# Bias sums dealt to a later stretch of each token group, and the first key weights split after the first group's input, in a two-layer GLA and stick-breaking kernel

## The chip, the core and the metric

The kernel runs on one NeuronCore of one Trainium2 chip. The metric is the device time of one execution in microseconds (us); lower is better. Five engines work beside one another and each takes its own instructions in order: TensorE (PE, with PEld for its weight loads), VectorE (DVE), ScalarE (ACT), GpSimd (POOL), and SyncE (SP), which issues nearly all transfers.

## The reference

There are 2048 tokens of 1024 features, in float32. Layer 0 is gated linear attention with 4 heads, layer 1 is stick-breaking attention with 16 heads whose keys and values come from a second modulated norm of the same stream. Every norm is scaled and shifted by vectors computed from a condition `c`.

```python
def ada_modulate(c, w, b, n):
    cond = jax.nn.silu(c) @ w + b
    return jnp.split(cond[:, None, :], n, axis=-1)
...
    proj = h @ w_in
    q, k, v, g, gk_lr = jnp.split(proj, GLA_SPLITS, axis=-1)
    gk = jax.nn.log_sigmoid((gk_lr @ w_gk2 + b_gk).astype(f32)) / GLA_GATE_NORMALIZER
...
    o = rms_norm(o, o_gain).reshape(bsz, seq, GLA_VAL_DIM) * jax.nn.silu(g.astype(f32))
    return o.astype(h.dtype) @ w_out
...
    q, g = jnp.split(h @ w_in, 2, axis=-1)
```

## The kernel before, in words

**Precision.** A weight or an activation is kept as two pieces, a high one made by ACT (`AF.Copy` into the rounded type) and a low one made by DVE (value less high piece). A product is then three matmuls (`mm3`, lines 142 to 144). `load_split` (L116 on ACT, L117 on DVE) does this to a weight block of two halves, each of which is one transfer `wr_*` issued by SP and two tiles `wh_*` and `wl_*` from a pool of ten (`wsp`).

**Layer 0** goes through four token groups of 512 (`g` = 0 to 3). For each group and each of 4 heads, `qkv` makes value, key and query projections (`pv`, `pk`, `pq`), `gate` the decays, `gla` the attention, `out_gate` the gate projection (`pg`), and `out_proj` the output (`py`). Within `gla`, the squares of the head's output are summed on ACT and DVE (`ss_o`, L192 to L196), and `rstd` feeds the sum to one matmul on PE (`ms_o`, L211), which stands five steps after the squares whatever the engines do meanwhile. While a group's first heads are projected, `normed_out` finishes the group before (`x` L577, `x1n` L222 and L223, stored by SP as `xn`).

**Bias sums.** In groups 2 and 3 `bias_sums` computes what the norm's shift adds to layer 1's projections: for each of 8 head pairs it loads the pair's weights in two halves (`wb`, issued by SP at L672), sums them on DVE over 8 rows of weights (`bs`, L686 once and L688 seven times), and `total` adds up over the partitions: two PE transposes (`pb`, L665) and one DVE reduction into `biases` (L667). Group 2 does the key and value weights, group 3 the query and gate weights. The `wb` tiles come from the same pool `wsp` as the weight pieces, and `pb` takes a bank of the same pool of four (`pl`) as `pv`, `pk`, `pq`, `ms_o` and `py`.

**What sets the order.** PE's order is the order of the program text: `play` advances the main work one step at a time (a step is usually three or six matmuls) and after each step each side job that was given to `spawn(gen, delay, every)`: it starts `delay` steps later and moves once in `every` steps. The other engines' orders are made by a list scheduler with priorities, in which work under `urgent()` goes early and work under `relaxed(n)` goes late; the bias sums are under `relaxed(200)`. Only `start()` is written out for all of PE, ACT, DVE and SP: there the text's order holds. It computes the first group's condition and its normed input `h_0` to `h_7` (`scaled`, L330 and L331; low piece L339). Weights are fetched one block ahead: `next_weight` takes the one in the list `ahead` and appends the next.

Of the kernel before, what the change touches and what calls it, by code (L numbers as in the profile page):

```python
# [1 line left out]

# [32 lines left out]
def yoco_kernel(ctx: ExitStack, tc: tile.TileContext, I: dict, O: dict):  # L35
# [20 lines left out]
    def t2(name, dt=F32):  # L56
        return m2.tile([P, TG], dt, tag="m2", name=name)
# [147 lines left out]
    def rstd(name, sq, mean, n=TG):  # L205


        ms = bank(po, f"ms_{name}")[:, 0:n]
        sq = sq if isinstance(sq, list) else [sq]
        for i, x in enumerate(sq):  # L210
            nc.tensor.matmul(ms, mean, x, start=i == 0, stop=i == len(sq) - 1)  # L211
        r = t2(f"r_{name}")[:, 0:n]
        q = t2(f"rq_{name}")[:, 0:n]
        nc.scalar.activation(r, ms, AF.Ln, bias=epsc)
        nc.scalar.activation(r, r, AF.Exp, scale=-0.5)
        nc.scalar.activation(q, r, AF.Square)
        nc.vector.scalar_tensor_tensor(q, ms, epsc, q, op0=ALU.add, op1=ALU.mult)
        nc.vector.scalar_tensor_tensor(r, q, -3.0, r, op0=ALU.add, op1=ALU.mult)
        return r
# [6 lines left out]
    def ada_rows(name, w, j, pool):  # L226

        acc = t4(f"aa_{name}_{j}", [P, D])
        for kt in range(KT):
            raw = pool.tile([P, D], F32, tag=pool.name, name=f"wa_{name}_{j}_{kt}")  # L230
            nc.sync.dma_start(raw, w[kt * P:(kt + 1) * P, j * D:(j + 1) * D])
            s = s_col[:, kt:kt + 1]
            if kt == 0:
                nc.vector.tensor_scalar(acc, raw, s, None, op0=ALU.mult)
            else:
                nc.vector.scalar_tensor_tensor(acc, raw, s, acc, op0=ALU.mult, op1=ALU.add)
            yield
        return acc
# [33 lines left out]
    def load_x(g, i, name="x"):  # L272
        t = t4(f"{name}_{g}_{i}", [P, 2, TG])
        nc.sync.dma_start(t, I["x"][g][:, 2 * i:2 * i + 2, :])
        return [t[:, 0], t[:, 1]]
# [24 lines left out]
    def start():  # L300

        T = start_group(0)
        w = I["w_ada"][0]
        rows = [ada_rows("l0", w, j, act) for j in range(2)]
        xs, sq = [], []
        for i in range(4):
            xs += load_x(0, i)
            for kt in (2 * i, 2 * i + 1):
                sq.append(t2(f"sq_x0_{kt}"))
                nc.scalar.activation(sq[kt], xs[kt], AF.Square)  # L310
        for _ in range(6):
            next(rows[0])
        r = rstd("x0", sq, mean_d)
        cond, pcs = new_cond("l0", 2), []
        for j in range(2):
            acc = result(rows[j])
            if j:
                gate_weights()
                ahead.append(next(blocks))
            pcs.append(bank(po, f"pc_l0_{j}"))  # L320
            ada_sum(pcs[j], acc)
        for j in range(2):
            cols = slice(8 * j, 8 * j + 8)
            nc.vector.tensor_tensor(cond[:, cols], pcs[j][:, 0:8], b_ada[:, cols], op=ALU.add)
        a, b = mods["l0m"] = modulation("l0", norm_gain[:, 0:8], cond)

        def scaled(kt):
            h = new_h(0, kt)
            xn = t2(f"xn_0_{kt}")
            nc.vector.scalar_tensor_tensor(xn, xs[kt], a[:, kt:kt + 1], r, op0=ALU.mult, op1=ALU.mult)  # L330
            nc.scalar.activation(h[:, 0], xn, AF.Identity, bias=b[:, kt:kt + 1])  # L331
            return h, xn

        ready = [scaled(0)]
        for kt in range(KT):
            if kt + 1 < KT:
                ready.append(scaled(kt + 1))
            h, xn = ready[kt]
            nc.vector.scalar_tensor_tensor(h[:, 1], xn, b[:, kt:kt + 1], h[:, 0].bitcast(F32),  # L339
                                           op0=ALU.add, op1=ALU.subtract)  # L340
            T.hs.append((h[:, 0], h[:, 1]))
        return T


# [241 lines left out]
    def start_group(g):  # L586
        T = Piece()
        T.g, T.hs, T.G, T.on, T.sg, T.og = g, [], {}, {}, {}, []
        return T
# [16 lines left out]
    blocks = weight_blocks()  # L606
    ahead = []

    def next_weight():
        if not ahead:  # L610
            ahead.append(next(blocks))
        w = ahead.pop()
        n = next(blocks, None)
        if n is not None:
            ahead.append(n)
        return w

    sides = []
# [1 line left out]
    def spawn(gen, delay=0, every=1):  # L620

        sides.append([gen, delay, every])
        return gen
# [32 lines left out]
    def bias_sums(i):  # L656


        which, m = (("w_kv", "kvm"), ("w_qg", "l1m"))[i]
        b = mods[m][1]  # L660

        def total(p, acc):
            pb = bank(po, f"pb_{i}_{p}")[:, 0:2 * P]
            for j in range(2):
                nc.tensor.transpose(pb[:, j * P:(j + 1) * P], acc[:, j * P:(j + 1) * P], ident)  # L665
            at = 4 * p + 2 * i
            nc.vector.tensor_reduce(biases[:, at:at + 2], pb.rearrange("p (j t) -> p j t", j=2),  # L667
                                    axis=mybir.AxisListType.X, op=ALU.add)

        def load(p, hf):  # L670
            raw = wsp.tile([P, 4, 256], F32R, tag="wsp", name=f"wb_{i}_{p}_{hf}").bitcast(F32)
            nc.sync.dma_start(raw, I[which][p][:, 4 * hf:4 * hf + 4, :])  # L672
            return raw

        seq = [(p, hf) for p in range(SBP) for hf in range(2)]
        raw, before = load(*seq[0]), None
        for n, (p, hf) in enumerate(seq):
            yield
            if hf == 0:
                acc = t2(f"bs_{i}_{p}")[:, 0:2 * P]  # L680
            with relaxed(200):
                for j in range(4):
                    kt = 4 * hf + j
                    s = b[:, kt:kt + 1]
                    if kt == 0:
                        nc.vector.tensor_scalar(acc, raw[:, j], s, None, op0=ALU.mult)  # L686
                    else:
                        nc.vector.scalar_tensor_tensor(acc, raw[:, j], s, acc, op0=ALU.mult, op1=ALU.add)  # L688
            if hf == 0 and before:
                total(*before)  # L690
            before = p, acc
            if n + 1 < len(seq):
                raw = load(*seq[n + 1])
        yield
        total(*before)

    def layer0():
        with tc.manual_schedule(engines={PE, ACT, DVE, mybir.EngineType.SP}):
            T = start()
        after = iter(())  # L700
        slow = ada("g0", I["w_ada"][0], b_ada, 2, 1)
        for g in range(NG):
            T.ready = 0
            first = qkv(T, 0)
            for _ in gate_low_rank(T):
                if g == 0:
                    next(first)
            spawn(slow, 1, 9)
            spawn(call(gate, T, 0), 3)
            spawn(after, 10, 2)  # L710
            extra = spawn(bias_sums(g - 2), 10, 12) if g > 1 else iter(())
            mix, gat = spawn(heads(T)), spawn(gates(T))
            N = start_group(g + 1) if g + 1 < NG else None
            for h, g_h in ((0, ()), (1, ()), (2, (0,)), (3, (1, 2, 3))):
                if h + 1 < GH:
                    spawn(call(gate, T, h + 1), 14)
                yield from first if h == 0 else qkv(T, h)
                spawn(is_ready(T), 6)
                for i in g_h:
                    if i == 2 and N:  # L720
                        spawn(squares_in(N), 8, 1)
                    yield from out_gate(T, i)
            run(mix)
            run(gat)
            into = normed_in(N) if N else prepare_pair(0)
            spawn(into, 2, 4 if N else 3)
            yield from out_proj(T)
            run(into)
            run(slow)
            run(extra)  # L730
            after = normed_out(T)
            if g == 0:
                slow = ada("kv", I["kv_w_ada"], kv_b_ada, 0, 2)
            if g == 1:
                mods["kvm"] = modulation("kv", kv_gain, mods["kv"])
                slow = ada("l1", I["w_ada"][1], b_ada[:, 24:48], 0, 3)
            if g == 2:
                mods["l1m"] = modulation("l1", norm_gain[:, 8:16], mods["l1"])
                mods["g1"] = mods["l1"][:, 16:24]
            T = N  # L740
        last.append(after)
# [391 lines left out]
```

## Time and profile before

| | |
|---|---|
| median of 3 runs | 2678.39 us (2674.71 to 2679.36) |
| the profiled execution | 2672.68 us |
| its span in the trace | 2670.9 us |
| mean granted TensorE clock | 0.987 of full speed |
| PE, DVE, ACT busy | 97%, 80%, 57% of the span |

The span is what the trace shows; about 2 us lie around it. Layer 0 takes the first 970 us or so, group 2 starts near 500 us and group 3 near 745 us. Since PE is busy nearly all the time, its idle time, and the time after it in which its clock is low, are what a change of order can take away or add.

### The profile page before, as it was taken

The page shows a single profiled execution, that of the slowest core. Times are in us where ns is not written, and L with a number is a line of the kernel's source. Part 1 is how long each engine was busy: PE and PEld are TensorE (multiplying, and loading weights), DVE is VectorE, ACT ScalarE, POOL GpSimd, SP SyncE. Part 2 cuts the span into 40 slices and gives each one's busy share as a digit, 9 for nine tenths or more (in the row PEclk, how much of TensorE's full clock was granted, in tenths as well). Part 3 has the DMA queues.
Part 4 walks back from the last instruction along what each step waited for, and adds up shares of the span by engine and source line. Part 5 has one row for each costly group of instructions (what it writes and reads, how often), then busy time and mean ns, then how long its engine had stood idle before and what let it go on. Part 6 is the DMA issues. An engine that isn't in the chain of part 4 may idle for free.

```text
span 2670.9 us, 38228 instructions
## 1 busy us (share of the span) xinstructions
PE 2595.8 (97%) x14008; PEld 2183.2 (82%) x14008; DVE 2124.6 (80%) x2941; ACT 1518.9 (57%) x2674; POOL 148.6 (6%) x346
## 2 busy tenths in 40 slices
PE   6999999989998999999999999999999999999998
PEld 4888888878787887888888888888888888887887
DVE  7657767687867657988988988989889889889866
ACT  4646756564575435655655556556556556566644
POOL 0000000000000001101001010010010010010000
PEclk7999999989999999999999999999999999999999
DMA  7326445555744475424332333325243233413464
GB/s 256 111 83 209 150 150 174 189 177 172 252 156 158 142 250 204 146 76 150 111 124 110 131 115 117 140 80 172 81 150 107 83 143 111 146 64 123 152 212 145
DMA packets 121292, 388.70 MB, mean 146 GB/s; under 512 B 14384, under 2 KB 18608, under 8 KB 121104
## 3 DMA queue, kind: packets, MB, share of 16 engines
q1 hardware_dynamic: 121104, 386.25, 42.0%
q8 instruction: 111, 1.82, 0.3%
q14 instruction: 77, 0.63, 0.1%
HBM read 328.52 MB, written 40.89 MB: 138 GB/s over the span
## 4 chain that ended last, share of the span: by engine, by line
PE 85%; DVE 7%; ACT 3%; DMA 3%; issue 1%; SPq 0%; DVEq 0%; ACTq 0%
PE pt L869 9%; PE o L887 5%; PE z L853 5%; PE o L886 5%; PE z L852 4%; PE lk L142 2%; PE lq L142 2%; PE lk L143 2%; PE lk L144 2%; PE lg L142 2%; PE lq L143 2%; PE lq L144 2%; PE pg L142 2%; PE lg L143 2%; PE lg L144 2%; PE pf L142 2%
## 5 line engine op out<-in xcount | busy, mean ns | idle before, releaser
L872 ACT ACTIVATE sh<-pt 128x512 fp32r<-128x512 f32 (+3 forms) x640 | 340.8, 533 | 526.3 <-PE pt L869 516.6
L873 DVE SCALAR_TENSOR_TENSOR sl<-pt,sh 128x512 fp32r<-128x512 f32 (+3 forms) x640 | 385.4, 603 | 147.0 <-ACT sh L872 140.8
L861 DVE TENSOR_TENSOR_SCAN S<-S,S 128x512 f32<-128x512 f32 x384 | 490.3, 1277 | 8.9 <-ACT S L856 7.2
L869 PE MATMUL pt<-ident,S 128*128 128x128 f32 x2176 | 344.1, 273 | 7.6 <-DVE sl L873 7.6
L856 ACT ACTIVATE S<-z 128x512 f32<-128x512 f32 (+3 forms) x640 | 339.5, 531 | 14.5 <-PE o L887 5.7
L869 PEld LDWEIGHTS pt<-ident,S 128*128 128x128 f32 x2176 | 271.1, 140 | 82.5 <-DVE sl L873 13.6
L852 PE MATMUL z<-k,q 128*128 128x512 f32 (+3 forms) x640 | 283.4, 443 | 0.2 <-ACT S L856 0.2
L887 PE MATMUL o<-sl,v 128*128 128x512 f32 (+3 forms) x640 | 233.8, 365 | 0.0
L853 PE MATMUL z<-k,ql 128*128 128x512 f32 (+3 forms) x640 | 233.5, 365 | 0.0
L886 PE MATMUL o<-sh,v 128*128 128x512 f32 (+3 forms) x640 | 230.4, 360 | 0.0
L861 DVE TENSOR_TENSOR_SCAN S<-S 128x128 f32<-128x128 f32 (+3 forms) x256 | 209.6, 822 | 18.1 <-POOL S L858 14.7
L437 PE MATMUL pv<-wh_v,h 128*128 128x256 f32 x512 | 156.8, 306 | 0.0
L858 POOL TENSOR_SCALAR_AFFINE_SELECT S<-S 128x128 f32<-128x128 f32 x256 | 87.0, 340 | 1229.1 <-ACT S L856 1209.0
L439 PE MATMUL pv<-wh_v,h 128*128 128x256 f32 x512 | 146.1, 285 | 0.0
L438 PE MATMUL pv<-wl_v,h 128*128 128x256 f32 x512 | 146.0, 285 | 0.0
L886 PEld LDWEIGHTS o<-sh,v 128*128 128x128 f32 x640 | 120.4, 188 | 28.3
L887 PEld LDWEIGHTS o<-sl,v 128*128 128x128 f32 x640 | 120.6, 188 | 26.5
L852 PEld LDWEIGHTS z<-k,q 128*128 128x128 f32 x640 | 121.9, 190 | 6.6 <-ACT S L856 0.5
L853 PEld LDWEIGHTS z<-k,ql 128*128 128x128 f32 x640 | 123.4, 193 | 0.2
L142 PE MATMUL pg<-h,wh_g 128*128 128x512 f32 x256 | 112.9, 441 | 0.0
L142 PE MATMUL lv<-xb,wh_w_kv 128*128 128x512 f32 x256 | 104.8, 409 | 3.9 <-DMA xb<-xn 3.9
L142 PE MATMUL lg<-xb,wh_w_qg 128*128 128x512 f32 x256 | 104.6, 409 | 0.0
(265 smaller groups left out, 6320.1 us busy)
## 6 DMA issues: line engine op xcount, KB each, us to landing
xb<-xn SPq DMA_DIRECT2D x256, 512.0 KB, 5.6
wa_l<-in_w_ada_dram SPq DMA_DIRECT2D x40, 512.0 KB, 6.2
wr_f<-in_w_out_dram SPq DMA_DIRECT2D x40, 512.0 KB, 3.8
x<-in_x_dram SPq DMA_DIRECT2D x32, 512.0 KB, 7.1
wr_v<-in_w_v_dram SPq DMA_DIRECT2D x32, 512.0 KB, 4.4
wr_kq<-in_w_kq_dram SPq DMA_DIRECT2D x32, 512.0 KB, 4.1
wr_g<-in_w_g_dram SPq DMA_DIRECT2D x32, 512.0 KB, 4.0
wr_out<-in_w_out_dram SPq DMA_DIRECT2D x32, 512.0 KB, 3.8
```

Of the source, the lines that this page charges most:

```text
L142: nc.tensor.matmul(out, hi, x[kt][0], start=first and i == 0, stop=False)
L143: nc.tensor.matmul(out, hi, x[kt][1], start=False, stop=False)
L144: nc.tensor.matmul(out, lo, x[kt][0], start=False, stop=last and i == end)
L852: nc.tensor.matmul(z, L.q[:, h, tcol], k[:, h, 0:w], start=True, stop=False)
L853: nc.tensor.matmul(z, L.ql[h][:, tcol], k[:, h, 0:w], start=False, stop=True)
L856: nc.scalar.activation(s, z, AF.Sigmoid, scale=-SCALE_B)
L861: nc.vector.tensor_tensor_scan(s[:, ::-1], s[:, ::-1], s[:, ::-1], 1.0 if diag else self.before.S[tb][:, 0:1], ALU.mult, ALU.min)
L869: nc.tensor.transpose(pt[:, tb * P:(tb + 1) * P], self.S[tb][:, sb * P:(sb + 1) * P], ident)
L872: nc.scalar.activation(hi, pt[:, t0 * P:], AF.Copy, bias=-1.0)
L873: nc.vector.scalar_tensor_tensor(lo, pt[:, t0 * P:], -1.0, hi.bitcast(F32), op0=ALU.add, op1=ALU.subtract)
L886: nc.tensor.matmul(o, v, hi, start=self.diag and sb == 0, stop=False)
L887: nc.tensor.matmul(o, v, lo, start=False, stop=self.c == 0 and sb == 3)
```

## The change

It has three parts.

1. `start()` ends by fetching the second weight block, the first key and query weights, so that the two ACT copies and two DVE subtractions of that split stand in the fixed order, behind `h_7`. Before, the block was fetched by the first call of `next_weight`, outside of the fixed order, and the scheduler placed it. `next_weight` now takes from the front of the list and fetches only when the list is empty; the fetches after that run one block ahead as before.
2. The bias sums start 40 steps into groups 2 and 3 and not 10, and move once in 9 steps and not in 12.
3. `total` of a pair is called after the second half of the next pair and not after its first half: the transposes of a pair come one move later behind its sums.

Nothing is added to or taken from the instructions of any engine.

```diff
--- before.py
+++ after.py
@@ -339,6 +340,7 @@
             nc.vector.scalar_tensor_tensor(h[:, 1], xn, b[:, kt:kt + 1], h[:, 0].bitcast(F32),
                                            op0=ALU.add, op1=ALU.subtract)
             T.hs.append((h[:, 0], h[:, 1]))
+        ahead.append(next(blocks))
         return T
@@ -609,10 +611,9 @@
     def next_weight():
         if not ahead:
             ahead.append(next(blocks))
-        w = ahead.pop()
-        n = next(blocks, None)
-        if n is not None:
-            ahead.append(n)
+        w = ahead.pop(0)
+        if not ahead:
+            ahead.extend(itertools.islice(blocks, 1))
         return w
@@ -686,9 +687,10 @@
-            if hf == 0 and before:
+            if hf and before:
                 total(*before)
-            before = p, acc
+            if hf:
+                before = p, acc
             if n + 1 < len(seq):
                 raw = load(*seq[n + 1])
         yield
@@ -708,7 +710,7 @@
-            extra = spawn(bias_sums(g - 2), 10, 12) if g > 1 else iter(())
+            extra = spawn(bias_sums(g - 2), 40, 9) if g > 1 else iter(())
```

**How the rows move.** In the names below, the last number of a tile is its buffer, the ones ahead of it are group, head or pair, and half; line numbers of the changed kernel are one or two higher.

Place 1 is the end of `start()` on DVE, the sequence that makes the first group's input. Before:

```order
L263 SCALAR_TENSOR_TENSOR a_l0_258<-cond_l0_186,vecs_97 128x8
L117 TENSOR_TENSOR wl_kq0_0_0_307<-wr_kq0_0_0_304,wh_kq0_0_0_306 128x1024
L330 SCALAR_TENSOR_TENSOR xn_0_0_261<-x_0_0_127,a_l0_258,r_x0_179 128x512
L330 SCALAR_TENSOR_TENSOR xn_0_1_265<-x_0_0_127,a_l0_258,r_x0_179 128x512
L117 TENSOR_TENSOR wl_kq0_0_1_313<-wr_kq0_0_1_310,wh_kq0_0_1_312 128x1024
L339 SCALAR_TENSOR_TENSOR h_0_0_260<-xn_0_0_261,cond_l0_186,h_0_0_260 128x512
L330 SCALAR_TENSOR_TENSOR xn_0_2_270<-x_0_1_133,a_l0_258,r_x0_179 128x512
L339 SCALAR_TENSOR_TENSOR h_0_1_264<-xn_0_1_265,cond_l0_186,h_0_1_264 128x512
L330 SCALAR_TENSOR_TENSOR xn_0_3_275<-x_0_1_133,a_l0_258,r_x0_179 128x512
L117 TENSOR_TENSOR wl_v0_1_0_473<-wr_v0_1_0_470,wh_v0_1_0_472 128x1024
L339 SCALAR_TENSOR_TENSOR h_0_2_269<-xn_0_2_270,cond_l0_186,h_0_2_269 128x512
```

With the change the sequence begins and ends as follows:

```order
L264 SCALAR_TENSOR_TENSOR a_l0_258<-cond_l0_186,vecs_97 128x8
L331 SCALAR_TENSOR_TENSOR xn_0_0_261<-x_0_0_127,a_l0_258,r_x0_179 128x512
L331 SCALAR_TENSOR_TENSOR xn_0_1_265<-x_0_0_127,a_l0_258,r_x0_179 128x512
L340 SCALAR_TENSOR_TENSOR h_0_0_260<-xn_0_0_261,cond_l0_186,h_0_0_260 128x512
L331 SCALAR_TENSOR_TENSOR xn_0_2_270<-x_0_1_133,a_l0_258,r_x0_179 128x512
```

```order
L340 SCALAR_TENSOR_TENSOR h_0_6_289<-xn_0_6_290,cond_l0_186,h_0_6_289 128x512
L340 SCALAR_TENSOR_TENSOR h_0_7_294<-xn_0_7_295,cond_l0_186,h_0_7_294 128x512
L118 TENSOR_TENSOR wl_kq0_0_0_303<-wr_kq0_0_0_300,wh_kq0_0_0_302 128x1024
L118 TENSOR_TENSOR wl_kq0_0_1_309<-wr_kq0_0_1_306,wh_kq0_0_1_308 128x1024
L383 TENSOR_TENSOR lr_0_380<-plr_0_313,lr_0_380 32x512
```

Three weight subtractions, two of the key weights and one of the second value weights (`wl_v0_1_0`), have left the stretch between `a_l0` and `h_7`; ACT's copies of the same three have left it too.

Place 2 is the first head of group 2 at its norm, on PE and DVE. PE before, and with the change:

```order
L438 MATMUL pv_2_2_0_4717<-wl_v2_2_1_4575,h_2_5_3899 128x256
L439 MATMUL pv_2_2_0_4717<-wh_v2_2_1_4574,h_2_5_3899 128x256
L665 MATMUL pb_0_1_4775<-ident_86,bs_0_1_4518 128x128 x2
L211 MATMUL ms_o2_0_4781<-ss_o2_0_4735,mean_v_91 128x512
L437 MATMUL pv_2_2_0_4717<-wh_v2_2_1_4574,h_2_6_3937 128x256
```

```order
L440 MATMUL pv_2_2_0_4700<-wl_v2_2_1_4551,h_2_5_3899 128x256
L441 MATMUL pv_2_2_0_4700<-wh_v2_2_1_4550,h_2_5_3899 128x256
L212 MATMUL ms_o2_0_4760<-ss_o2_0_4718,mean_v_91 128x512
L439 MATMUL pv_2_2_0_4700<-wh_v2_2_1_4550,h_2_6_3937 128x256
L440 MATMUL pv_2_2_0_4700<-wl_v2_2_1_4551,h_2_6_3937 128x256
```

DVE before, and with the change:

```order
L577 TENSOR_TENSOR x1_1_3_4003<-x1_1_3_4003,r_y1_4506 128x512
L196 TENSOR_TENSOR ss_o2_0_4735<-ss_o2_0_4735,sq_o2_0_1_4737 128x512
L223 TENSOR_TENSOR x1n_1_5_4655<-x1_1_2_3922,x1n_1_5_4655 128x512
L223 TENSOR_TENSOR x1n_1_6_4666<-x1_1_3_4003,x1n_1_6_4666 128x512
L577 TENSOR_TENSOR x1_1_3_4003<-x1_1_3_4003,r_y1_4506 128x512
L117 TENSOR_TENSOR wl_kq2_2_0_4707<-wr_kq2_2_0_4704,wh_kq2_2_0_4706 128x1024
L236 SCALAR_TENSOR_TENSOR aa_l1_0_4108<-wa_l1_0_7_4724,s_col_100,aa_l1_0_4108 128x1024
L223 TENSOR_TENSOR x1n_1_7_4683<-x1_1_3_4003,x1n_1_7_4683 128x512
L688 SCALAR_TENSOR_TENSOR bs_0_1_4518<-wb_0_1_0_4403,cond_kv_2173,bs_0_1_4518 128x256
```

```order
L579 TENSOR_TENSOR x1_1_3_4003<-x1_1_3_4003,r_y1_4493 128x512
L118 TENSOR_TENSOR wl_kq2_2_0_4690<-wr_kq2_2_0_4687,wh_kq2_2_0_4689 128x1024
L237 SCALAR_TENSOR_TENSOR aa_l1_0_4108<-wa_l1_0_7_4707,s_col_100,aa_l1_0_4108 128x1024
L224 TENSOR_TENSOR x1n_1_7_4666<-x1_1_3_4003,x1n_1_7_4666 128x512
L687 TENSOR_SCALAR bs_0_0_4566<-wb_0_0_0_4434,cond_kv_2173 128x256
L689 SCALAR_TENSOR_TENSOR bs_0_0_4566<-wb_0_0_0_4434,cond_kv_2173,bs_0_0_4566 128x256
L687 TENSOR_SCALAR bs_0_1_4735<-wb_0_1_0_4657,cond_kv_2173 128x256
L689 SCALAR_TENSOR_TENSOR bs_0_0_4566<-wb_0_0_0_4434,cond_kv_2173,bs_0_0_4566 128x256
L197 TENSOR_TENSOR ss_o2_0_4718<-ss_o2_0_4718,sq_o2_0_1_4720 128x512
```

On PE the second pair's transposes no longer stand ahead of `ms_o`; the first pair's, which stood 118 rows ahead of them, now come 46 rows behind `ms_o`, after the next head's four `pkt` transposes and six more `pv` matmuls. On DVE `ss_o`, on which `ms_o` waits, has moved from a place ahead of `x1n_5` to one behind `x1n_7` and four bias-sum operations. ACT's two squares for it (`ss_o`, `sq_o`) now stand behind its last copy `x1n_7` as well. In group 3 the rows at the same place move alike, without `aa_l1` and with three bias-sum operations ahead of `ss_o`, all of the first pair.

Place 3 is the start of group 2's output projection on PE. Before, and with the change:

```order
L665 MATMUL pb_0_6_5757<-ident_86,bs_0_6_5572 128x128 x2
L142 MATMUL pg_2_3_1_5730<-h_2_7_3955,wh_g2_3_1_5514 128x512
L143 MATMUL pg_2_3_1_5730<-h_2_7_3955,wh_g2_3_1_5514 128x512
L144 MATMUL pg_2_3_1_5730<-h_2_7_3955,wl_g2_3_1_5515 128x512
L142 MATMUL py_2_0_5791<-og_2_0_0_5157,wh_out02_0_0_5659 128x512
```

```order
L144 MATMUL py_2_0_5795<-og_2_0_1_5161,wh_out02_0_0_5672 128x512
L145 MATMUL py_2_0_5795<-og_2_0_1_5161,wl_out02_0_0_5673 128x512
L666 MATMUL pb_0_7_5803<-ident_86,bs_0_7_5655 128x128 x2
L143 MATMUL py_2_0_5795<-og_2_1_0_5530,wh_out02_0_0_5672 128x512
L144 MATMUL py_2_0_5795<-og_2_1_0_5530,wh_out02_0_0_5672 128x512
```

The last pair's transposes, 65 rows further on before, now stand behind the first six `py` matmuls, nine matmuls behind the place where the seventh pair's stood. Their bank is the one that `ms_o` of the fourth head held, so they also wait for DVE's last read of it (`rq_o`, L217 before, L218 now).

## Rows read from the trace of the kernel before

**Rows 1.** The page, part 1: busy time of PE, share of the span, instructions.
```profile
PE 2595.8 (97%) x14008; PEld 2183.2 (82%) x14008; DVE 2124.6 (80%) x2941; ACT 1518.9 (57%) x2674; POOL 148.6 (6%) x346
```
**Rows 2.** The waits of PE: who waited for whom, us in total, times, longest.
```profile
PE pb L665 <- DVE bs L688: 20.1, 5, 8.3
...
PE plr L373 <- ACT h L331: 4.0, 1, 4.0
...
PE ms_x L211 <- DVE sg L536: 0.8, 1, 0.8
PE pk L142 <- DVE biases L667: 0.7, 1, 0.7
```
**Rows 3.** Timeline of PE, groups 2 and 3: start, us, instruction [idle before].
```profile
538.35 0.51 PE L665 MATMUL pb<-ident,bs 128*128 128x128 f32 x2 [2.53 <-DVE bs L688]
...
570.96 0.66 PE L665 MATMUL pb<-ident,bs 128*128 128x128 f32 x2 [8.32 <-DVE bs L688]
571.42 1.92 PE L211 MATMUL ms_o<-ss_o,mean_v 128*128 128x512 f32 x2
...
580.71 0.60 PE L479 MATMUL pkt<-ident,kf 128*128 128x128 f32 x4
...
710.34 0.44 PE L665 MATMUL pb<-ident,bs 128*128 128x128 f32 x2 [1.22 <-DVE bs L688]
...
814.71 0.66 PE L665 MATMUL pb<-ident,bs 128*128 128x128 f32 x2 [7.74 <-DVE bs L688]
815.16 1.91 PE L211 MATMUL ms_o<-ss_o,mean_v 128*128 128x512 f32 x2
```
**Rows 4.** Table of windows: stretch, length, busy per engine, granted clock, DMA share.
```profile
42.00:47.00 5.00, 4.76 (x17) 3.54 (x18) 4.16 (x6) 2.28 (x3) 0.00 (x0) 0.50 0.32 116
...
539.00:542.00 3.00, 3.00 (x11) 2.60 (x10) 2.12 (x5) 1.40 (x3) 0.00 (x0) 0.50 0.86 287
...
571.00:575.00 4.00, 4.00 (x13) 2.74 (x13) 1.19 (x3) 3.80 (x4) 0.00 (x0) 0.50 0.60 229
```
**Rows 5.** Timeline of DVE in start().
```profile
37.10 1.22 DVE L117 TENSOR_TENSOR wl_kq<-wr_kq,wh_kq 128x1024 fp32r<-128x1024 f32 x1
38.24 1.41 DVE L330 SCALAR_TENSOR_TENSOR xn<-x,a_l,r_x 128x512 f32<-128x512 f32 x2
...
51.10 1.63 DVE L339 SCALAR_TENSOR_TENSOR h<-xn,cond_l,h 128x512 fp32r<-128x512 f32 x2
```
**Rows 6.** Timeline of ACT in start().
```profile
38.85 1.06 ACT L116 ACTIVATE wh_kq<-wr_kq 128x1024 fp32r<-128x1024 f32 x1 [2.04 <-DMA wr_kq<-in_w_kq_dram]
39.82 1.32 ACT L331 ACTIVATE h<-xn,cond_l 128x512 fp32r<-128x512 f32 x2
```
**Rows 7.** Timeline of DVE in group 2, at the first head's norm.
```profile
559.78 0.68 DVE L196 TENSOR_TENSOR ss_o<-ss_o,sq_o 128x512 f32<-128x512 f32 x1
560.39 1.29 DVE L223 TENSOR_TENSOR x1n<-x,x1n 128x512 fp32r<-128x512 f32 x2
...
564.53 0.68 DVE L223 TENSOR_TENSOR x1n<-x,x1n 128x512 fp32r<-128x512 f32 x1
565.13 0.48 DVE L688 SCALAR_TENSOR_TENSOR bs<-wb,cond_kv,bs 128x256 f32<-128x256 f32 x1
565.52 0.35 DVE L686 TENSOR_SCALAR bs<-wb,cond_kv 128x256 f32<-128x256 f32 x1
565.79 1.67 DVE L688 SCALAR_TENSOR_TENSOR bs<-wb,cond_kv,bs 128x256 f32<-128x256 f32 x4
```
**Rows 8.** Timeline of DVE in group 3, same place.
```profile
808.93 0.68 DVE L223 TENSOR_TENSOR x1n<-x,x1n 128x512 fp32r<-128x512 f32 x1
```
**Rows 9.** Timeline of ACT in group 3, behind the first head's norm.
```profile
817.83 1.28 ACT L215 ACT_TABLE_LOAD   x1
819.12 0.63 ACT L215 ACTIVATE r_o<-r_o 128x512 f32<-128x512 f32 x1
```
**Rows 10.** Transfers of the output weights (wr_out), issue to landing.
```profile
DMA to landing us min/median/max: 3.1/3.8/10.8
```

More of the change, by code (lines that the diff above doesn't have):

```diff
@@ L1 @@
+import itertools
 from contextlib import ExitStack, nullcontext
```

## The prediction

> **What bounds the kernel now.** I read the page's busy times first: PE is busy 97% of the span [rows 1], so the other engines' orders matter only where they make PE wait. The list of PE's waits says where [rows 2]: the largest entry is `pb`, the transposes of the bias sums, five waits and 20.1 us; the wait of the first group's low-rank matmul `plr` for ACT's first `h` is 4.0. The entries that the change does not reach (the condition of `start()`, layer 1) are not shown. PE's timeline then gives the five `pb` waits one by one [rows 3]: 2.53, 8.32 and 1.22 in group 2, 7.74 in group 3; the fifth is the 0.31 that is left of 20.1. The two long ones stand directly ahead of `ms_o`, the matmul of the first head's norm. The windows show what a wait costs beyond itself: the granted clock is 0.50, so 1.2 of 2.4 GHz, in the 3 us behind the wait of 2.53 and in the 4 us behind that of 8.32 [rows 4].
>
> **Part 1, the first key weights.** DVE has `a_l` ready at 37.1 and then does a subtraction of key weights of 1.22 before the first `xn` at 38.24 [rows 5]. ACT, after a wait of 2.04 for a transfer, copies the second half of those weights at 38.85, and only then makes `h_0` at 39.82 [rows 6], for which PE waits [rows 2]. Now `xn_0` starts at 37.1 and takes 0.75, so ACT can start `h_0` at about 37.9 and PE at about 38.6: 1.9 to 2.0 earlier. Further on, the subtractions of `wl_kq` and `wl_v` (1.14 each as they follow one another, 38.24 less 37.10) leave the chain of `xn` and `h`, which then runs at 0.66 apiece. `h_0`'s low piece goes from about 38.6, seven more steps of 1.32 follow, and `h_7` is done at about 48.6, not 52.7 (51.10 plus 1.63) [rows 5]. That would be 4; but PE runs at the low clock at first [rows 4], and eight matmuls per step then take about 2.1 us, so three or four steps are bound by PE itself. I take **3.0**, between 2.0 (the first `h` alone) and 4.0 (the last). The cover: the moved key split (two subtractions, 2.3) is done by about 51, and PE needs it only behind the second half of the first value projection, 48 matmuls or more than 5 us after `h_7`; without that cover the 2.3 would be given back. The second value block, whose split now follows, is needed a key and a query projection later still; I cost it at nothing.
>
> **Part 2, group 2.** The transposes of pairs 0 and 1 leave the places at which PE waited 2.53 and 8.32. That does not return the sum of the two, since something else becomes late: `ss_o`. It was done at 559.78 plus 0.68 [rows 7], in time, and is now queued on DVE behind `x1n_5` to `x1n_7` and four bias operations (place 2). By the rows: DVE finished `x1n_7` at 565.13 [rows 7]. Without `ss_o` in front of it (0.61, from 559.78 to 560.39) and with the chain starting 2.5 to 2.9 earlier, because PE delivers `pk` of the second head without the wait of 2.53 and most of the low clock behind it, that becomes about 561.7. Four bias operations (0.27 and 0.39 apiece, by the starts 565.13, 565.52, 565.79: two of each, 1.3) and `ss_o` itself give **563.5**. PE gets there at 557 to 558.5: 562.64, where the old wait of 8.32 began, less 2.53, the 1.5 that the 3 us at half clock lost, and the transposes. So a **new wait of 5 to 6.5 us** stands at `ms_o`, its releaser DVE's `ss_o`. `ms_o` itself goes from 571.42 [rows 3] to 563.5: **7.9** gained, and the low clock behind it remains as it was. Bound from above: with no wait at `ms_o`, 13 to 14; from below: nothing, if DVE's backlog is 8 us longer than I make it.
>
> Pair 0's sums are needed next. From `ms_o` to the end of the next `pkt` and six `pv` matmuls is 10.6 us (571.42 to 580.71 [rows 3] plus 1.3), so PE comes to `pb_0` at about 574.1. The last of its sums stands behind `rq_o` and `r_o` of this norm: `ms_o` at 563.5, about 2 until ACT reads it, logarithm, table, exponential and square at 0.65, 1.28, 0.63 and 0.63 [rows 9], then about 2.1 of DVE work: 570.9. It is covered by 3.
>
> **Part 2, group 3.** The same, without `aa_l1`. There `x1n_7` was done at 809.54 [rows 8, 7] and the chain starts between 0 and 1.0 earlier (the waits of 0.31 and 0.7 ahead of it go); I take 0.5. Less `ss_o`'s 0.61, plus one bias operation and `ss_o` behind it (two stood ahead of `x1n_7` and still do), it is ready at about **809.5**. PE is there at 805.7 (814.71 less 7.74, the 0.31, the 0.7 of `pk` for `biases` [rows 2] and the transposes). A wait of 3.8 remains, and `ms_o` goes from 815.16 [rows 3] to 809.5: **5.6** gained. Bounds: 9.4 and 0.
>
> **The last pair, and the queues.** At the end of groups 2 and 3, `pb_7` stands 65 rows earlier (place 3) and also waits for DVE's `rq_o` of the fourth head, which now has the two subtractions of the second output block ahead of it, 2.3. The wait of 1.22 and `ms_x`'s of 0.8 [rows 2, 3] go; if about half of the 2.3 is covered by PE's own way there, 1 to 2 takes their place in group 2, and the same can arise in group 3, where nothing was. I book 0, between 2.0 gained and 3 lost for both groups. Moving `total` back by one move is what gives the other pairs' sums their cover, so I book nothing for it. SP issues `wb` loads at other places; the ones that come ahead of weights (`wr_v` and `wr_kq` of the fourth head, `wr_out`) wait for sums that, by the order, are some moves old by then; I book 0, and take what it could cost as rival (c).
>
> On tables the profile shows ACT's second load in `rstd` done in 1.28, with the next instruction 0.01 behind it [rows 9]. The Trainium skill, "ScalarE: Activation LUTs", section "What ACT_TABLE_LOAD costs", gives about 1.38 us of drain on top of that for every switch of set. By that rule `rq_o` would come 1.4 to 2.8 later, `pb_7` would wait that much longer in both groups, and the sum below would be 3 to 5 less. The row decides: no drain is seen there.
>
> **Sum.** 3.0 + 7.9 + 5.6 + 0 = **16.5** off the profiled execution of 2672.7, 0.6%. The median of the runs, 2678.4, lies 5.7 above that execution, so I take 16.5 off the median: **2662**.
>
> **Rivals.** (a) *No replacement wait.* DVE reaches `ss_o` before PE does, and all of `pb`'s 20.1, `pk`'s 0.7 and some 4 of low clock go, with 3 of part 1: 28, or about 2651. For it: `ss_o` was 1.5 us or more early before. Against: its place on DVE behind `x1n_7`, which ended at 565.13 with PE there at 562.64. (b) *The wait is only renamed.* The backlog at `ss_o` is as late as the sums were, for instance because the second pair's `wb`, which one of the operations ahead of it needs, lands late; then part 1 and a little remain: 3 to 5, about 2674. Between this and the forecast everything is possible by degrees. (c) *Slower.* The loads of the second output block `wr_out_1` are issued behind the last `wb` on SP, and the fourth head's `rq_o` stands behind that block's splits on ACT and DVE, with `pb_7` behind `rq_o` and all of the output projection behind `pb_7`. I put the block's landing some 5 us ahead of need, so it decides from there on; to come out 5.4 slower it has to cost 16.5 + 5.4 = 22, or 11 in each group. A landing took 3.8 in the median and 10.8 at worst [rows 10], so one late landing costs about 2 and the price needs SP blocked for some 12 us twice: about 2685. (d) *Part 1 does nothing*, because PE at the low clock is the bound there: 13.5, or 2665.
>
> **How the numbers follow.** Forecast with (d), 2656 to 2669: 0.66. (a): 0.12. (b): 0.17, of which 0.06 below the line of faster. (c): 0.05. A measurement of this kernel can tell about 0.2%, 5.4 us, so faster means under 2673.0: 0.66 + 0.12 + 0.06 = 0.84; same is the rest of (b), 0.11; slower 0.05. The range takes in the forecast, half of (a) and most of (b): 2653 to 2674.
>
> **What would show it.** Right: in `start()` no key-weight subtraction ahead of `xn_0`, PE's first `plr` near 38.6; in the list of PE's waits `pb` falls from 20.1 to below 4, and `ms_o` for `ss_o` appears with 5 to 6.5, ending at about 560.5 (563.5 less part 1's 3.0), and with 3.8, ending at about 798.6 (809.5 less 3.0 and 7.9); the clock falls to 0.50 behind the first at least. Wrong: `pb` still with waits above 4, `ms_o` missing from the list (a) or with waits of 8 and more (b), or a wait above 5 at `pb_7` or `py` (c).

## The result, and the profile after

The changed kernel takes 2663.3 us (median of 6 runs, 2660.4 to 2664.6) against 2678.45 for the kernel before (6 runs, 2672.5 to 2679.4). The ratio is 0.9946, 95% interval 0.9933 to 0.9959: 15.1 us faster in the medians, and by the interval between 11 and 18. The profiled executions are closer to each other, 2663.8 against 2672.7, that is 8.9, and the two spans differ by 8.8 (2662.1 against 2670.9). The steps below account for those 8.8; where the rest comes from is taken up with the third profile of the kernel before.

The list of PE's waits in the changed kernel, beside [rows 2] (waited for: us in total, times, longest):

```profile
PE ms_o L212 <- DVE ss_o L197: 12.3, 4, 6.1
...
PE psc L469 <- DVE e L459: 3.0, 2, 1.6
...
PE plr L375 <- ACT h L332: 2.0, 1, 2.0
PE pb L666 <- DVE rq_o L218: 1.5, 1, 1.5
...
PE ms_x L212 <- DVE sg L538: 0.2, 1, 0.2
```

The 20.1 us at `pb` for DVE's sums are gone, and the 0.7 of `pk` for `biases` too. In their place stand 12.3 at `ms_o` for `ss_o`, which had 0.2 before. PE's timeline of the changed kernel shows where, beside [rows 3]:

```profile
38.84 0.64 PE L375 MATMUL plr<-h,lrw 128*32 128x512 f32 x1 [2.00 <-ACT h L332]
...
524.40 0.49 PE L469 MATMUL psc<-e,gk 128*128 128x128 f32 x2 [1.62 <-DVE e L459]
563.59 2.08 PE L212 MATMUL ms_o<-ss_o,mean_v 128*128 128x512 f32 x2 [6.14 <-DVE ss_o L197]
676.94 1.10 PE L212 MATMUL ms_o<-ss_o,mean_v 128*128 128x512 f32 x2 [1.27 <-DVE ss_o L197]
687.28 0.44 PE L666 MATMUL pb<-ident,bs 128*128 128x128 f32 x2 [1.46 <-DVE rq_o L218]
...
805.61 2.08 PE L212 MATMUL ms_o<-ss_o,mean_v 128*128 128x512 f32 x2 [4.67 <-DVE ss_o L197]
```

The long waits of 8.32 and 7.74 became 6.14 and 4.67 at the next row of the program. DVE's timeline of the changed kernel at the first of them, beside [rows 7]:

```profile
560.81 0.68 DVE L224 TENSOR_TENSOR x1n<-x,x1n 128x512 fp32r<-128x512 f32 x1
561.41 0.34 DVE L687 TENSOR_SCALAR bs<-wb,cond_kv 128x256 f32<-128x256 f32 x1
561.79 0.48 DVE L689 SCALAR_TENSOR_TENSOR bs<-wb,cond_kv,bs 128x256 f32<-128x256 f32 x1
562.19 0.35 DVE L687 TENSOR_SCALAR bs<-wb,cond_kv 128x256 f32<-128x256 f32 x1
562.45 0.48 DVE L689 SCALAR_TENSOR_TENSOR bs<-wb,cond_kv,bs 128x256 f32<-128x256 f32 x1
562.85 0.68 DVE L197 TENSOR_TENSOR ss_o<-ss_o,sq_o 128x512 f32<-128x512 f32 x1
```

No row has an idle time in front of it: DVE works without a break in this stretch, and `ss_o` stands in line behind `x1n_7` and four bias operations. The table of windows of the changed kernel shows the clock behind the waits at `psc` and `ms_o` of group 2, and at the start of group 3, where only the 0.31 at `pc_l` (733.78) stands ahead (the figure ahead of the last two is the granted clock, as in [rows 4]):

```profile
525.00:528.00 3.00, 3.00 (x15) 2.59 (x15) 2.52 (x3) 3.00 (x8) 0.00 (x0) 0.56 0.73 216
564.00:567.00 3.00, 3.00 (x10) 1.97 (x9) 2.65 (x5) 1.28 (x2) 0.00 (x0) 0.50 0.96 333
735.00:738.00 3.00, 3.00 (x16) 1.75 (x16) 2.88 (x4) 1.03 (x1) 0.00 (x0) 0.83 0.75 199
```

Matching rows of PE's timeline in the two traces gives how far the changed kernel is ahead at each place, in us. Here `ms_y` is the norm matmul of the group that is being finished (`normed_out`), and `pc_kv` and `pc_l` are the sums of layer 1's conditions; `psc` above is a head's scores, which need DVE's scaled queries `e`.

| place | before | after | ahead |
|---|---|---|---|
| `ms_o`, first head, group 0 | 107.39 | 104.14 | 3.25 |
| `pc_kv`, end of group 1 | 459.91 | 456.56 | 3.35 |
| `ms_y` in group 2 | 534.70 | 534.13 | 0.57 |
| `ms_o`, first head, group 2 | 571.42 | 563.59 | 7.83 |
| `ms_o`, second head, group 2 | 607.39 | 600.50 | 6.89 |
| `pc_l`, end of group 2 | 739.52 | 733.78 | 5.74 |
| `ms_y` in group 3 | 781.97 | 777.61 | 4.36 |
| `ms_o`, first head, group 3 | 815.16 | 805.61 | 9.55 |
| `ms_o`, fourth head, group 3 | 923.53 | 914.37 | 9.16 |
| end of the span | 2670.9 | 2662.1 | 8.8 |

### The profile page after: what moved, and what is told of

It reads as the page before. It is cut to its first block, busy times and chain, and to the rows that moved or that the text cites. A ratio compares the mean times of both kernels' runs of the same rounds, so it can differ in the third digit from the quotient of the medians.

```text
span 2662.1 us, 38238 instructions
## 1 busy us (share of the span) xinstructions
PE 2595.3 (97%) x14008; PEld 2183.6 (82%) x14008; DVE 2124.4 (80%) x2941; ACT 1518.3 (57%) x2674; POOL 149.1 (6%) x346
## 4 chain that ended last, share of the span: by engine, by line
PE 66%; DVE 5%; DMA 2%; ACT 1%; issue 1%; SPq 0%; DVEq 0%; ACTq 0%
PE pt L871 9%; PE o L889 5%; PE z L855 5%; PE o L888 4%; PE z L854 4%; PE lk L143 2%; PE lq L143 2%; PE lk L144 2%; PE lk L145 2%; PE lg L143 2%; PE lq L144 2%; PE lq L145 2%; PE lg L144 2%; PE lg L145 2%; PE lv L143 2%; PE lv L144 2%
## 5 line engine op out<-in xcount | busy, mean ns | idle before, releaser
L439 PEld LDWEIGHTS pv<-wh_v,h 128*128 128x128 f32 x512 | 99.4, 194 | 6.7 <-issue 2.8
```

Source lines behind the costliest of these rows:

```text
L439: nc.tensor.matmul(o, xh, hi, start=i == 0, stop=False)
```

## The experiments

My theory was that part 1 is worth 3 us by itself, and that in groups 2 and 3 PE's waits follow from the place of `ss_o` and of the sums in DVE's order against the place of `pb` on PE. The rival was that DVE has too much to do in that stretch, whatever the order, and a wait moved only shows at the next instruction. There are ten runs in three sessions, each session on another chip: eight variants, and the kernel before twice. Each variant is compared with the runs of the kernel before in its own session (medians 2676.6, 2675.3 and 2674.9), so what two variants of different sessions differ by is read from their ratios.

**The first part alone.** In the changed kernel, the sums as before:

```diff
-            if hf and before:
+            if hf == 0 and before:
                 total(*before)
-            if hf:
-                before = p, acc
+            before = p, acc
...
-spawn(bias_sums(g - 2), 40, 9)
+spawn(bias_sums(g - 2), 10, 12)
```

> Only the first part of the change: the key split behind h_7 and the new next_weight; the bias sums as before. My theory: the first plr starts near 38.8 us, everything behind is 3.0 to 3.4 us earlier up to group 2, and the bias waits stay as they were (pb about 20 us in five waits, no ms_o wait above 0.5): 2675, 3.3 us or 0.12% faster. Rival: the 3.3 us are taken back at the first pb waits, because those wait for transfers and DVE work that do not start earlier: 2678, no change.

Measured: 2671.1, ratio 0.9982 (0.9973 to 0.9990), 3 to 7 us faster. Its list of waits:

```profile
PE pb L666 <- DVE bs L689: 20.5, 5, 8.4
...
PE plr L375 <- ACT h L332: 2.0, 1, 2.0
```

The gain of part 1 is in the times. The profile, of the slowest of the eleven runs (2674.9, a span of 2673.2), does not show it to the end. PE is 3.1 ahead of the first profile of the kernel before at `ms_o` of the first head (104.27 against 107.39) and 0.1 ahead at `ms_y` in group 1 (309.14 against 309.20), well before any bias wait: the clock is low behind the wait of 1.59 at `psc` in group 1 (298.01), and in the first profile it was not. One window, and the long `pb` wait:

```profile
300.00:304.00 4.00, 4.00 (x18) 3.54 (x18) 3.45 (x5) 3.62 (x7) 0.00 (x0) 0.50 0.58 193
...
571.04 0.66 PE L666 MATMUL pb<-ident,bs 128*128 128x128 f32 x2 [8.36 <-DVE bs L689]
```

The third profile of the kernel before (the last run below) has low clock at the same place. Against it PE is 1.83 ahead at the first `pb` of [rows 3] (538.40 against 540.23) and 1.81 at the second (571.04 against 572.85). The bias waits take nothing back, so the rival falls. What is lost comes later: 0.8 is left at `pc_l` at the end of group 2 (740.51 against 741.29), and behind it comes a stretch of low clock that the other profile does not have. This kernel has no wait at `psc` in group 2.

**The two parts on the sums alone.** `ahead.append(next(blocks))` is taken out of `start()`, and `next_weight` is the old one.

> Only the two parts on the bias sums; start() as before. My theory: the first plr at 40.6 us again, pb waits near 1.5, and ms_o waits of about 6 and 4.7 us in groups 2 and 3 with DVE's ss_o as the releaser: 12 us faster, 2666 to 2667. On the wait of 1.6 us at psc in group 2 (524.4 us): if it stays, the bias sums' move made it; if it goes, PE's earlier arrival through the first part made it, and then this kernel is nearer to 2665.

Measured: 2665.0, ratio 0.9959 (0.9946 to 0.9973), 7 to 14 us faster. Its list of waits:

```profile
PE ms_o L212 <- DVE ss_o L197: 11.5, 4, 6.1
...
PE psc L468 <- DVE e L458: 3.1, 2, 1.5
```

The two halves of the change add up within the intervals (4.8 and 11.0 by the ratios, against 14.5 for the whole). The wait at `psc` in group 2, 1.53 at 527.72, stays without part 1: the two parts on the sums made it.

**The third part undone.** In the changed kernel:

```diff
-            if hf and before:
+            if hf == 0 and before:
                 total(*before)
-            if hf:
-                before = p, acc
+            before = p, acc
```

> The changed kernel with its third part undone: total is again called after the first half of the next pair, with the sums dealt from step 40 in every 9. In its order pb of pair 0 stands 19 rows ahead of ms_o, as pb of pair 1 did in the kernel before, while DVE's order is the changed one. My theory: the third part is what gives the sums their cover, so PE waits at that pb until DVE has done all of pair 0, about 10 to 12 us in group 2 and 8 to 10 in group 3, and the time rises to 2668 to 2674. Rival: dealing the sums later was enough by itself; then the waits stay at ms_o (6 and 4.7) and the time at 2662 to 2665.

Measured: 2677.2, ratio 1.0008 (0.9999 to 1.0017), no faster than before the change. PE's timeline:

```profile
568.90 0.69 PE L666 MATMUL pb<-ident,bs 128*128 128x128 f32 x2 [12.72 <-DVE bs L689]
...
815.65 0.69 PE L666 MATMUL pb<-ident,bs 128*128 128x128 f32 x2 [11.40 <-DVE bs L689]
```

The waits come where the theory has them, a little longer, and the time lies 3 above its range. Dealing the sums later, without calling `total` later, loses about what part 1 brings.

**The second part undone.** In the changed kernel:

```diff
-spawn(bias_sums(g - 2), 40, 9)
+spawn(bias_sums(g - 2), 10, 12)
```

> The changed kernel with its second part undone: the sums start at step 10 and move every 12 steps, as before, but total comes one move later. pb of pair 0 then stands 66 rows ahead of ms_o and pb of pair 1 77 rows behind it, and ss_o of the first head stands early on DVE, with no weight split or bias operation between it and its squares. My theory: the waits at pb and at ms_o both fall below 2 us, psc in group 2 does not wait, and the kernel is faster than the changed one: 2650 to 2656. The second part would then cost more than it brings. Rival: DVE's work in that stretch is too much in any order, and the wait returns at pb of pair 0 or at ms_o with 4 us or more: 2660 to 2666.

Measured: 2652.5, ratio 0.9915 (0.9902 to 0.9929), 19 to 26 us faster. PE's timeline, the two longest waits of groups 2 and 3:

```profile
572.78 0.41 PE L666 MATMUL pb<-ident,bs 128*128 128x128 f32 x2 [3.35 <-DVE bs L689]
...
698.23 0.44 PE L666 MATMUL pb<-ident,bs 128*128 128x128 f32 x2 [2.81 <-DVE bs L689]
```

`ms_o` of the first heads does not wait, nor does `psc` in group 2. The waits of 3.35 and 2.81 are above my 2, but the time is in the forecast range. So the third part alone, beside part 1, is worth more than the whole change, and the second part costs about 8 us by the ratios (0.9915 against 0.9946; the medians, of two sessions, differ by 10.8).

**`ms_o` later on PE.** The change as it is, and in `gla`:

```diff
-        for _ in range(5):
+        for _ in range(12 if T.g > 1 and h == 0 else 5):
             yield
         r = rstd(f"o{n}", ss, mean_v)
```

> The changed kernel with ms_o of the first head in groups 2 and 3 seven steps later on PE (12 steps behind the squares and not 5); DVE's order up to ss_o is the same. pb of pair 0 then stands a few rows ahead of ms_o. My theory: PE has 5 us of other work while DVE gets to ss_o, so the waits in that stretch fall from 6.1 and 4.7 to about 1.3 and 1, and the time by 8 to 11 us, to 2652 to 2656. Rival: DVE's backlog is only shown at the next instruction that needs it, pb of pair 0: waits of 4 us or more there, and 2660 to 2664.

Measured: 2679.0, ratio 1.0012 (1.0003 to 1.0021): a miss, 15 above the rival's range and slower than the kernel before. PE's timeline in group 2:

```profile
566.44 0.69 PE L666 MATMUL pb<-ident,bs 128*128 128x128 f32 x2 [6.24 <-DVE bs L689]
586.32 1.22 PE L496 MATMUL po<-sc,v 128*128 128x128 f32 x4 [5.51 <-POOL sc L477]
```

The wait is as long as it was and stands at `pb`, as the rival has it, and a second one of 5.5 comes behind, for the second head's `sc`. ACT's timeline of this kernel shows why:

```profile
569.82 0.69 ACT L215 ACTIVATE r_o<-ms_o,epsc 128x512 f32<-128x512 f32 x1 [9.41 <-PE ms_o L212]
...
584.99 0.57 ACT L475 ACTIVATE sc<-psc 128x512 f32<-128x512 f32 x1
```

The same row in the changed kernel:

```profile
572.87 0.60 ACT L475 ACTIVATE sc<-psc 128x512 f32<-128x512 f32 x1 [3.38 <-PE psc L470]
```

ACT waits 9.41 for the later `ms_o`. The edit also changed ACT's order: in the changed kernel `sc` stands ahead of the next head's gate (`e` from 578.03 on), here behind it (`e` from 575.25, `gk` at 582.86), though its `psc` was done by 575.4. So this run moved more than PE's row, and it does not tell what a later `ms_o` alone would do.

**The sums dealt still later, and faster.** The change with `spawn(bias_sums(g - 2), 60, 8)`.

> The changed kernel with the bias sums 60 steps in and every 8 steps, not 40 and 9. In its order ss_o of the first head stands ahead of x1n_5 again (group 2) or ahead of the last x (group 3), with no bias operation in front of it. My theory: the place of ss_o in DVE's queue is the cause of the ms_o waits, so they fall from 12.3 us to below 2 and the time falls by another 10 to 14 us with the low clock behind them: 2649 to 2654. Rival: DVE has too much to do in that stretch, and the wait comes back at another instruction (pb of the first pairs, psc, or the last pb_7, which now has less time): 2660 to 2665 with 8 us or more in waits at pb or psc.

Measured: 2649.2, ratio 0.9908 (0.9894 to 0.9923), 21 to 28 us faster. PE's timeline:

```profile
557.36 1.12 PE L212 MATMUL ms_o<-ss_o,mean_v 128*128 128x512 f32 x2 [0.31 <-DVE ss_o L197]
669.72 1.13 PE L212 MATMUL ms_o<-ss_o,mean_v 128*128 128x512 f32 x2 [2.51 <-DVE ss_o L197]
...
791.93 1.12 PE L212 MATMUL ms_o<-ss_o,mean_v 128*128 128x512 f32 x2 [1.04 <-DVE ss_o L197]
```

DVE's timeline of the same kernel, which does `ss_o` ahead of `x1n_5`:

```profile
556.61 0.69 DVE L197 TENSOR_TENSOR ss_o<-ss_o,sq_o 128x512 f32<-128x512 f32 x1
557.21 1.29 DVE L224 TENSOR_TENSOR x1n<-x,x1n 128x512 fp32r<-128x512 f32 x2
```

With `ss_o` back in its early place the waits of 6.14 and 4.67 are 0.31 and 1.04, at the same work on every engine. The sum over `ms_o` is 4.0 and not below 2, because the fourth head has 2.51. By itself this does not part the place of `ss_o` from the amount of work, since no bias operation at all comes ahead of `ss_o` in these two stretches now. The kernel with the second part undone does. There DVE does nine bias operations ahead of the first head's `ss_o` in each of the two groups, against four and three in the change, and still `ss_o` comes early; DVE's timeline of that kernel in group 2:

```profile
554.82 0.69 DVE L197 TENSOR_TENSOR ss_o<-ss_o,sq_o 128x512 f32<-128x512 f32 x1
```

That is 8 us ahead of the 562.85 of the change, with more bias work done, and `ms_o` does not wait. So the place of `ss_o`, and not the amount of work, made those two waits.

**Later by four more steps.** The change with `spawn(bias_sums(g - 2), 64, 8)`.

> The bias sums 64 steps in, every 8 steps; against 60 and 8 the first head's ss_o stands ahead of x1n_5 in group 3 too. Theory: the wait of 1.0 us at ms_o in group 3 goes, those of 2.5 at the fourth head's ms_o and 0.7 at pb of the last pair in group 2 stay or grow by 1, since the sums end four steps later: 2647 to 2651, no measurable difference to 60 and 8. Rival: the later end of the sums delays the output projection by more than 4 us: 2653 or more.

Measured: 2660.0, ratio 0.9945 (0.9932 to 0.9957): the rival. PE's timeline, the last pair in groups 2 and 3:

```profile
691.98 0.66 PE L666 MATMUL pb<-ident,bs 128*128 128x128 f32 x2 [6.27 <-DVE bs L689]
...
926.18 0.44 PE L666 MATMUL pb<-ident,bs 128*128 128x128 f32 x2 [4.62 <-DVE bs L689]
```

Four steps cost about 10 us by the ratios. At 60 and 8 DVE has the last pair's sums done in time (0.7 of wait at that `pb`, and for another operand); at 64 and 8 PE gets there first. It is the kind of wait that the kernel before had, at the other end of the group.

**`total` two moves later, the sums dealt as before the change.** In the kernel with the second part undone:

```diff
-            if hf and before:
-                total(*before)
+            if hf == 0 and len(done) > 1:
+                total(*done.pop(0))
             if hf:
-                before = p, acc
+                done.append((p, acc))
...
-        yield
-        total(*before)
+        for f in done:
+            yield
+            total(*f)
```

> The sums dealt as before the change (step 10, every 12) and total two moves later than before (one more than in the change), start() as changed. In its order pb of pair 1 stands 47 rows and pb of the last pair 36 rows further on than with total one move later, and ss_o of the first head stands early on DVE. My theory: what decides is the distance between a pair's last sum on DVE and its transposes on PE, without putting sums ahead of ss_o; the pb waits of 3.3, 2.8 and 1.8 us that are left with one move go, with the low clock behind two of them, and the time falls from 2652.5 to 2642 to 2647. Rival: those waits move to what comes next on PE or DVE (ms_o of the fourth head, py, or the next group's first projections, since the last pair now ends in the output projection): 2650 or more.

Measured: 2647.4 (2643.9 to 2653.2), ratio 0.9900 (0.9887 to 0.9914), 23 to 30 us faster: the lowest median here, 0.4 above the upper end of what was expected. PE's timeline:

```profile
702.22 0.41 PE L666 MATMUL pb<-ident,bs 128*128 128x128 f32 x2 [3.09 <-DVE bs L689]
...
823.03 1.12 PE L212 MATMUL ms_o<-ss_o,mean_v 128*128 128x512 f32 x2 [1.18 <-DVE ss_o L197]
```

The waits of 3.35 in group 2 and 1.79 in group 3 are gone; the last pair's in group 2 stays at 3.09, now a move later. Against 60 and 8 the intervals overlap, so which of the two is faster stays open. Both beat the change and the kernel before.

**The kernel before, twice more.**

> The kernel before, profiled once more, since its first profiled span (2670.9 us) lies 5.7 below the median of its runs while that of the changed kernel lies at its median. Theory A: the usual longer execution has more low-clock time behind the same waits (a span of 2676 to 2678 with the same five pb waits and the same 20 us in them, and a granted clock under 1.0 in a stretch that had 1.0 in the first profile). Theory B: the pb waits themselves are longer in the usual execution (23 us or more in sum), and the change takes them away. A span near 2671 again tells nothing.

Measured: 2672.15, a span of 2670.4: on the question asked it tells nothing, as said. One place of it bears on the next run. In group 1 `psc` waits longer here than in any other profile, and the clock stays up behind it:

```profile
300.18 0.49 PE L467 MATMUL psc<-e,gk 128*128 128x128 f32 x2 [2.17 <-DVE e L457]
...
301.00:304.00 3.00, 3.00 (x23) 2.62 (x24) 2.40 (x4) 3.00 (x8) 0.00 (x0) 1.00 0.81 242
```

> The kernel before, profiled a third time. Theory A: its waits at pb are again about 20 us, and its span differs from the others by stretches of low clock behind short waits (psc in group 1, pc_l in group 3), which come in some executions and not in others; a span of 2674 or more comes with at least one such stretch more than in the first profile. Theory B: a longer span comes with longer waits at pb.

Measured: 2674.5, a span of 2672.8, with 20.1 us in five `pb` waits as in [rows 2]. The difference lies in group 1. PE's timeline and one window of this execution:

```profile
299.90 0.49 PE L467 MATMUL psc<-e,gk 128*128 128x128 f32 x2 [1.55 <-DVE e L457]
...
301.00:304.00 3.00, 3.00 (x17) 2.66 (x15) 2.42 (x4) 3.00 (x8) 0.00 (x0) 0.59 0.78 254
```

The same place in the first profile of the same kernel:

```profile
300.95 0.49 PE L467 MATMUL psc<-e,gk 128*128 128x128 f32 x2 [1.65 <-DVE e L457]
...
302.00:305.00 3.00, 3.00 (x25) 2.62 (x24) 2.42 (x4) 3.00 (x7) 0.00 (x0) 1.00 0.76 266
```

A wait of the same length is followed by a low clock in one execution and by none in the other. In the third profile `psc` starts 1.05 earlier than in the first (299.90 against 300.95) and the next `ms_o` 1.85 later (334.56 against 332.71): it costs 2.9 us. That is the mechanism of theory A, though the span stays below the 2674 that it named; theory B falls, since the `pb` waits are as long as they were.

## Why the prediction was right, and where its steps were not

The time came out at 2663.3, 1.3 above the 2662 of the text and within its range; the sign and the main mechanism, the new wait, are as forecast. The steps hold less well than the total, and that the total is so near is partly luck, as the end of this section shows.

- *Part 1, 3.0.* Right: the first `plr` at 38.84 (38.6), its wait 4.0 down to 2.00, and 3.25 to 3.35 kept through groups 0 and 1. PE at the low clock did not eat it up, so rival (d) falls; that `h_7` ends near 48.4 (46.78 plus 1.63 on DVE), where 48.6 was forecast, shows the chain as worked out.
- *Group 2, 7.9.* The wait is there as forecast, with DVE's `ss_o` as its releaser and 6.14 long (5 to 6.5). The gain up to that row is only 4.5, 7.83 less the 3.35 that it had already. The step that failed is "the chain starting 2.5 to 2.9 earlier": PE lost 1.62 at `psc` and ran at 0.56 of its clock behind that, so the lead fell from 3.35 to 0.57 ahead of `ms_y`. For the same reason that wait ends at 563.6 and not at 560.5: DVE is through with `x1n_7` at 561.4, and the forecast, with part 1, has 558.7. I had followed the order of DVE from the second head's results on, and not from the start of the group. The runs put this on the second part: the wait is there in all kernels here whose sums start at step 40 or later, and in none whose sums start at step 10. The low clock behind it comes in three of those six profiles and not in the other three; from `psc` to `ms_y` it is 9.7 us with it and 8.2 to 8.3 without, so about 1.5 of the loss came by chance. Which rows of DVE make `e` late there was not followed up.
- *Group 3, 5.6.* 5.19 measured (9.55 less 4.36); the wait is 4.67 and not 3.8. It ends at 805.61 and not at about 798.6, because PE comes into this stretch 4.36 ahead and not 10.9 (3.0 and 7.9).
- *The rest of group 2, 0.* Mis-sized: 0.94 goes from the first head's `ms_o` to the second's (7.83 to 6.89), where I had the low clock behind the wait as it was. From the second head of group 2 to the end of that group 1.15 is lost (6.89 to 5.74). `pb_7` waits 1.46 for `rq_o`, as forecast (1 to 2), and the 1.22 and 0.8 are gone, but `ms_o` of the fourth head waits 1.27, which was not in the sum.
- *Low clock in group 3.* Between 5.74 and 4.36 no wait is longer than the 0.31 at `pc_l`, and the clock is at 0.83 behind it in the window from 735, while the same wait, 0.83 long, was followed by no such stretch in the first profile of before. Of the other eleven profiles the ones of part 1 alone and of the later `ms_o` have low clock at this place (from 743 and from 740), behind waits of 0.53 and 0.17. Nothing in the forecast had this.
- *"Moving `total` back by one move ... I book nothing for it."* This is the step that was most wrong as a reading of the change. The runs show it the other way round: the third part carries the whole gain in groups 2 and 3, and the second takes about half of it back (0.9982 with part 1 alone, 0.9915 with the third part beside it, 0.9946 with all three). Without the third, the kernel is at 2677; without the second, at 2652.5. My walk through the rows of the changed order had both parts in it; neither was priced by itself.
- *The tables.* No drain behind ACT's table loads is to be seen in the changed kernel either. ACT's timeline in group 3:

```profile
808.43 1.28 ACT L216 ACT_TABLE_LOAD   x1
809.73 0.63 ACT L216 ACTIVATE r_o<-r_o 128x512 f32<-128x512 f32 x1
```

The next instruction starts 0.02 behind the load. The 1.38 us of the Trainium skill, "ScalarE: Activation LUTs", "What ACT_TABLE_LOAD costs", do not show here, so none of what the sum lost is put down to them.

**The 15.1 and the 8.8.** The sum, 16.5, was worked out from the rows of the first profile, and against that profile the changed kernel is 8.8 ahead: the sum is 7.7 too much. Part 1 gave 0.35 more than booked. Group 2 up to `ms_o` gave 3.4 less and group 3 0.4 less. The rest of group 2 took 0.94 and 1.15, the stretch with low clock ahead of `ms_y` in group 3 took 1.38, and 0.75 went behind the first head of group 3. The forecast then took the 16.5 off the median of the runs, 5.7 above the profile, as if the changed kernel's profile would lie as far below its own median. It lies at it (2663.8 against 2663.3). A sum that was too large and an offset that did not last nearly cancel: that the time is only 1.3 off is luck.

How large the gain is depends on what is compared: 15.1 in the medians of its own session, and 16.5 lies in their interval of 11 to 18; 8.8 against the first profile and 10.7 against the third (2672.8 less 2662.1). Stretches of low clock behind short waits, 2.9 us in the one shown, lengthen some executions of the kernel before, and its first profile, at its low end, has none at that place; that they make up the whole rest is not shown. The changed kernel ran in that session only; against the medians of the kernel before in the three sessions of the experiments it would be 11.6 to 13.3 faster.

## What to carry to other kernels

Where work off the critical path must be handed to the bounding engine, what counts is the distance between its last operation on the helper engine and its reader on the bounding one; lengthening that distance (here one line that calls `total` a move later) brought the gain in groups 2 and 3, and moving the work alone brought none. Moving the work also changes what it is queued ahead of: look up, in the new order, which operation on the critical path now stands behind it, and count from the start of the stretch, not from the wait that is to go. And a delay has an end as well as a beginning: four steps too many brought the same wait back at the end of the group.

## What the runs showed of the hardware that was not expected

The low level of TensorE's clock (0.50 of full speed, 1.2 GHz) followed not only the long waits. In group 1 `psc` waits between 1.37 and 2.17 us in all twelve profiles. Behind it the clock fell in four of them, after waits of 1.53 to 1.59, and stayed up in eight, the longest wait of 2.17 among them. From this `psc` to the next head norm (`ms_o`) it is 31.8 us in those eight, 33.2 in two of the four and 34.7 in the other two, so such a stretch costs 1.5 or 2.9 us. What decides whether it comes is not in these traces: the length of the wait does not. In group 2 the picture is the same, with low clock behind `psc` in three of the six profiles that have the wait there and in none of the six that do not.

For reading a profile this means that two executions of one kernel can differ by a few us at a place that no edit touched, so a gain of that size is told from several times and not from one pair of profiles. A short wait on a busy TensorE can cost more than its length; what removing one is worth on average was not measured here.
